# Stores to DRAM scratch moved from SyncE's queue to GpSimd's in two stages of an encoder block

## The chip, the cores and the metric

The kernel runs on one core of a Trainium2 chip. The metric is the device time of one execution in microseconds; the figure given for a kernel is the median over its runs. The engines are called TensorE (PE in the profile, PEld for its weight loads), VectorE (DVE), ScalarE (ACT), GpSimd (POOL) and SyncE (SP). SyncE computes nothing here; it issues DMAs.

## The reference

One layer of a hybrid bidirectional encoder on x of 1 x 1024 x 1024 float32. Branch A is gated linear attention in both directions with 4 heads; branch B is windowed attention with 8 query heads and 2 key heads in blocks of 128. Both are projected, gated and summed, go through W_out, and a SwiGLU block with a hidden width of 2816 follows.

```python
h = _rms_norm(x, norm_mix_g[l])
proj = h @ w_in[l]
(g_q, g_k, g_v, g_r, g_lr_f, g_lr_b, s_q, s_k, s_v, gate_a, gate_b) = jnp.split(proj, split_at, axis=-1)
y_gla = _gla_branch(g_q, g_k, g_v, g_r, g_lr_f, g_lr_b, ...) @ w_o_gla[l]
y_swa = _swa_branch(s_q, s_k, s_v, ...).astype(x.dtype) @ w_o_swa[l]
merged = jax.nn.sigmoid(gate_a) * y_gla + jax.nn.sigmoid(gate_b) * y_swa
x = x + merged @ w_out[l]
h2 = _rms_norm(x, norm_ffn_g[l])
gu = h2 @ w_ffn_in[l]
x = x + (jax.nn.silu(gu[..., :D_FF]) * gu[..., D_FF:]) @ w_ffn_out[l]
```

## The kernel before, in words

Float32 accuracy is had by splitting each operand into a high part (type fp32r, made on ScalarE) and the rest (made on VectorE), and doing three matmuls: high by high, high by low, low by high. So each weight unit of 128 x 512 costs a DMA, a ScalarE copy, a VectorE subtraction and matmuls. Larger products are done by a seven-product scheme on 2 x 2 blocks (the sets 11, 21, 22, T1 to T4), whose operands are sums and differences of blocks. Little stays in SBUF: projections, operand sums and attention outputs are stored to scratch tensors in DRAM and loaded again when they are needed.

The stages in order of time:

- The norm of x, and the first q and k projections (the block from line 352).
- The GLA stage (the block from line 697). `g_gates`, `g_decays`, `g_parts`, `g_scores`, `g_out`, `g_back_out` and `g_turn` work on pairs of 128-token chunks. They load q and k (lines 435, 436) and v (486) from scratch; `g_turn` stores its two transposed heads (594). Between them `fill(n)` draws matmuls from a list of dense projections: `proj_f` (q, k; stored by `proj_f_out`, line 142), `proj_t` (v, and the windowed attention's kv and q; line 227), whose weight units are loaded by `wunit` (65) and, in `wkeep` (162), stored again in split form so that the second half of the tokens can load them in `wagain` (170, 175). `next_unit` keeps AHEAD = 2 units beyond the one in use. In the same time `all_sums` makes operand sums on VectorE and stores them with `put` (116).
- The SWA stage (the block from line 945): `prep`, `a_rope`, `k_turn`, `a_turn`, `a_scores` (the masked scores, 831), `a_soft`, `a_probs` (the transposed probabilities are split into ph and pl, 873 and 874) and `a_out`, which stores the output of four heads through `heads(...)` (885). `heads` is a view of a scratch tensor of 128 x 2048 that picks 128 tokens of each of four heads, so one store writes four rows of 128 numbers per partition. The dense list goes on with `proj_t` and ends with `first_halves` (products of the branch gates, evacuated on VectorE in line 254, stored in 257). When the attention runs out, `drained(t)` loads finished outputs (`b_load`, 892) and makes their sums in place (`b_sum`, 898), which are stored through `heads` too (899). The tiles that `b_load` fills are the attention's own buffers (tags qr, sq, rq, kvr); qr has two.
- The pair stage (line 1123 on), branch projections, W_out and the feed-forward part. Their stores stay where they are.

Order: PE's instructions are issued in the order of the program text (`manual_schedule`). The order on the other engines and queues is made by the framework's planner from its own estimates; a queue then runs in that order, and an instruction that waits holds what stands behind it. All semaphores are set by the framework. Before the change every DMA is issued from SyncE's queue. Staging tiles (`stage()`, tag st) rotate over four buffers, weight tiles wh and wl over five, wr over four; a buffer is written again only when its store has landed. The program reserves scratch for DMAs issued by GpSimd:

```python
nc = _bacc.Bacc("TRN2", target_bir_lowering=False, num_devices=1, dynamic_dma_scratch_size=1024)   # line 1739
```

Of the kernel before, what the change touches and what calls it, by code (L numbers as in the profile page):

```python
# [8 lines left out]
F32 = mybir.dt.float32  # L9
# [5 lines left out]
P = 128  # L15
# [15 lines left out]
def body(tc, i, out):  # L31
    nc = tc.nc
    with ExitStack() as root:
# [12 lines left out]
        def mmtile(shape=(P, 512), dt=F32):  # L46
            return psm.tile(list(shape), dt, tag="mm", name=nm("mm"))
# [4 lines left out]
        def scratch(name, shape=(P, 512)):  # L52
            return dram.tile(list(shape), F32, tag=name, name=name)

        def stage(shape=(P, 512), dt=F32):
            return stg.tile(list(shape), dt, tag="st", name=nm("st"))
# [15 lines left out]
        def mm(o, a, b, start, stop):  # L72
            nc.tensor.matmul(o, a, b, start=start, stop=stop)  # L73
# [36 lines left out]
        xl = [[xp.tile([P, HT], FR, tag=f"xl{k}{s}", name=f"xl{k}{s}") for s in range(2)] for k in range(KT)]  # L110

        scr = {}

        def put(key, t):
            d = scratch("_".join(map(str, key)))
            nc.sync.dma_start(out=d, in_=t)
            scr[key] = d

        swks = ExitStack()
# [13 lines left out]
        def proj_f_out(name, b):  # L133
            for s in range(2):
                d = scratch(f"{name}_{s}")
                t = stage()
                if name[0] == "q":
                    nc.vector.scalar_tensor_tensor(t, b[s], 128 ** -0.5, rstd[:, s * HT:(s + 1) * HT],
                                                   op0=ALU.mult, op1=ALU.mult)
                else:  # L140
                    nc.vector.tensor_tensor(t, b[s], rstd[:, s * HT:(s + 1) * HT], op=ALU.mult)
                nc.sync.dma_start(out=d, in_=t)
                scr[name, s] = d


# [4 lines left out]
        def next_unit():  # L150
            while plan and len(ready) <= AHEAD:
                ready.append(plan.pop(0)())
            return ready.pop(0)
# [3 lines left out]
        def wkeep(n, k):  # L157
            h, l = wunit(i["w_t"][n, k])
            kept[n, k] = []
            for v, q in ((h, "h"), (l, "l"))[n < 2:]:  # L160
                d = dram.tile([P, 512], F32, tag=f"w{q}{n}_{k}", name=f"w{q}{n}_{k}")
                nc.sync.dma_start(out=d, in_=v.bitcast(F32))
                kept[n, k].append(d)
            return h, l

# [31 lines left out]

        def proj_t(name, n, s):
            plan.extend((lambda k=k: (wkeep, wagain)[s](n, k)) for k in range(KT))

            def steps():
                if True:
                    b = [mmtile() for _ in range(4)]
                    us = []

                    def unit_mm(k, t):
                        h, l = us[k]
                        c = slice(t * P, (t + 1) * P)
                        st, sp = k == 0, k == KT - 1
                        for x, w, f0, f1 in ((xh, h, st, False), (xh, l, False, False), (xl, h, False, sp)):  # L210
                            mm(b[t], x[k][s][:, c], w, f0, f1)
                            yield

                    for ks in ((0, 1), (2,), (3,), (4,), (5,)):
                        us.extend(next_unit() for _ in ks)
                        for t in range(4):
                            for k in ks:
                                yield from unit_mm(k, t)
                    us.extend(next_unit() for _ in range(2))
                    for t in range(4):  # L220
                        yield from unit_mm(KT - 2, t)
                        yield from unit_mm(KT - 1, t)
                        ti = s * 4 + t
                        d = scratch(f"{name}_{ti}")
                        o = stage()
                        nc.scalar.activation(o, b[t], AF.Copy, scale=rstdt[:, ti:ti + 1])
                        nc.sync.dma_start(out=d, in_=o)
                        scr[name, ti] = d
            return steps()

# [3 lines left out]
        def first_halves():  # L234
            for j in range(0, len(PAIRS), 2):
                for u in range(2):
                    plan.extend((lambda r=PAIRS[j + q][2], u=u: wunit(i["w_f"][r, u])) for q in range(2))

            def steps():
                for j in range(0, len(PAIRS), 2):  # L240
                    Y = [mmtile(), mmtile()]
                    for u in range(2):
                        for q in range(2):
                            nme, m = PAIRS[j + q][:2]
                            h, l = next_unit()
                            for kk in range(4):
                                k = u * 4 + kk
                                c = slice(kk * P, (kk + 1) * P)
                                for w, x, f0, f1 in ((h, xh[k][0], k == 0, False), (h, xl[k][0], False, False),
                                                     (l, xh[k][0], False, k == KT - 1)):  # L250
                                    nc.tensor.matmul(Y[q], w[:, c], x, start=f0, stop=f1, skip_group_check=True)  # L251
                                    yield
                            t = stage()
                            nc.vector.tensor_tensor(t, Y[q], rstd[:, 0:HT], op=ALU.mult)
                            key = (f"{nme}{m}", 0) if u else (f"{nme}{m}", "p1")
                            d = scratch("_".join(map(str, key)))
                            nc.sync.dma_start(out=d, in_=t)
                            scr[key] = d
            return steps()

# [2 lines left out]
        def fill(n):  # L263

            while n > 0 and dense:
                try:
                    next(dense[0])
                    n -= 1
                except StopIteration:
                    dense.pop(0)  # L270
# [315 lines left out]
        def g_turn(hd, c):  # L586
            a = gla.pop((hd, c))
            ot = chtile((P, 2, P))
            for j in range(2):
                nc.tensor.transpose(ot[:, j], a.ob[:, j * P:(j + 1) * P], ident)  # L590
            os_ = gtile("ot", (P, 2, P))
            nc.scalar.copy(os_, ot)
            for j in range(2):
                nc.sync.dma_start(out=scr["o", 2 * hd + j, c // 4][:, (c % 4) * P:(c % 4 + 1) * P], in_=os_[:, j])

        dense += [proj_t("v0", 0, 0), proj_t("v0", 0, 1), proj_f("q1", 2), proj_f("k1", 3), proj_f("q2", 4), proj_f("k2", 5),
                  proj_t("v1", 1, 0), proj_t("v1", 1, 1), proj_f("q3", 6), proj_f("k3", 7), *(proj_t(nme, n, s) for s in range(2)
# [86 lines left out]
        for n in range(NH * NC):  # L684
            hd, c = divmod(n, NC)
# [9 lines left out]
                behind[n + 1] = (g_parts, hd, c)  # L695
        sums = all_sums()
        with tc.manual_schedule(engines={mybir.EngineType.PE}):
            fill(44)
            for t in range(last + 1):
                work = [[at[t, j]] for j in (0, 5, 4, 3, 2, 1) if (t, j) in at]  # L700
                if t in behind:
                    work = work or [[]]
                    work[-1].append(behind[t])
                if t < 22 and work:
                    work[(len(work) - 1) // 2].append((next, sums, None))
                slot([lambda v=v: [f(*a) for f, *a in v] for v in work], share(GF, t))
                next(sums, None)
# [37 lines left out]
        def heads(q, n):  # L745
            return groups[q].rearrange("p (h t) -> p h t", h=4)[:, :, n % 4 * P:(n % 4 + 1) * P]
# [130 lines left out]
        def a_out(g, n):  # L877
            a = att.pop((g, n))
            o = chtile((P, 4, P))
            for kb, ph, pl in a.pts:  # L880
                mm3(o, vSh[kb][:, g * P:(g + 1) * P], vSl[kb][:, g * P:(g + 1) * P], ph, pl,
                    kb == a.b0, kb == a.b1)
            ob = stage((P, 4, P))
            nc.scalar.copy(ob, o)
            nc.sync.dma_start(out=heads(f"b{g + 1}{n // 4 + 1}", n), in_=ob)

        loaded = {}

# [5 lines left out]
        def b_sum(n, *js):  # L894
            a, b, c, d = loaded[n]
            for j in js:
                q, t, x, y = (("bT1", b, b, a), ("bT2", c, c, b), ("bT3", a, c, a), ("bT4", d, d, c))[j]
                nc.vector.tensor_tensor(t, x, y, op=ALU.subtract)
                nc.sync.dma_start(out=heads(q, n), in_=t)

        def drained(t):
            if t in (0, 2):
# [30 lines left out]
        for n in range(2 * KT):  # L933
            t, g = divmod(n, 2)
# [10 lines left out]
        with tc.manual_schedule(engines={mybir.EngineType.PE}):  # L945
            for t, v in enumerate(todo):
# [5 lines left out]
                if a_scores in names:  # L952
                    pin = a_turn in names and t < 5
                    k = names.index(a_turn) if pin else max(j for j, f in enumerate(names) if f is a_scores)
                    g = v[names.index(a_scores)]
# [165 lines left out]
                 (("12", 1), ("sum2", 3)), (("22", 1), ("21", 1)), (("11", 2),), (("12", 2), ("22", 2)), (("21", 2), ("11", 3)), (("12", 3), ("22", 3)), (), ())  # L1121

        with tc.manual_schedule(engines={mybir.EngineType.PE}):
            homes["T2"] = tp, "t2h{}", "t2l{}", 0
            for k in range(4):
                if k == 2:
# [12 lines left out]
            for j in range(0, len(PAIRS), 2):  # L1139
# [4 lines left out]
                v = [pair_T3(f) for f in two]  # L1144
# [606 lines left out]
```

## Time and profile before

| | |
|---|---|
| median of 3 runs | 1605.99 us (1605.62 to 1606.2) |
| the profiled execution | 1604.61 us |
| its span, first to last instruction | 1602.7 us |
| busy: PE, PEld, DVE, ACT, POOL | 1589.7, 1320.6, 1245.9, 928.4, 0.2 us |
| granted clock of TensorE | 1.00 |
| moved by DMA | 349.47 MB, 218 GB/s over the span |

In the profile L12 is line 12 of the kernel; a tile is named without its buffer number; "out<-in" says what an instruction writes and reads. An instruction of SyncE's queue is written SPq. Matmuls overlap, so a single one's duration is longer than the time from one to the next. "Landing" is the time from the issue of a DMA to the arrival of its semaphore.

### The profile page before, as it was taken

How to read it: one execution, taken by the hardware profiler on the slowest of the kernel's cores; microseconds unless marked ns; L12 is line 12 of the kernel's file. 1: busy time of each engine (PE TensorE's matmuls, PEld its weight loads, DVE VectorE, ACT ScalarE, POOL GpSimd, SP SyncE). 2: the span in 40 equal slices, each digit the busy share in tenths (PEclk: the TensorE clock that was granted, in tenths of full speed). 3: DMA queues.
4: the chain of work that ended last, by engine and by line, in shares of the span. 5: the costliest groups of instructions: out<-in, count | busy, mean ns of one | idle time of the engine just before them, and what ended most of it. 6: DMA issues, size and time to landing. Idle time of an engine off the chain costs nothing.

```text
span 1602.7 us, 23256 instructions
## 1 busy us (share of the span) xinstructions
PE 1589.7 (99%) x7484; PEld 1320.6 (82%) x7484; DVE 1245.9 (78%) x2355; ACT 928.4 (58%) x1911; POOL 0.2 (0%) x4
## 2 busy tenths in 40 slices
PE   9999999999999999999999999999999999999999
PEld 6888888887888788888888888888888888888887
DVE  8578898837899878876877987777777878689655
ACT  7555877864998745445665647844444444354442
POOL 0000000000000000000000000000000000000000
PEclk9999999999999999999999999999999999999999
DMA  7888877888555798877876777634344554695433
GB/s 263 294 273 266 267 250 261 279 273 296 176 155 152 242 301 292 285 239 262 277 232 211 229 219 219 197 113 150 112 150 153 194 200 164 207 331 174 150 99 118
DMA packets 223900, 349.47 MB, mean 218 GB/s; under 512 B 24255, under 2 KB 67135, under 8 KB 223778
## 3 DMA queue, kind: packets, MB, share of 16 engines
q1 hardware_dynamic: 223778, 347.99, 66.6%
q8 instruction: 59, 0.97, 0.3%
q14 instruction: 63, 0.52, 0.1%
HBM read 235.17 MB, written 112.73 MB: 217 GB/s over the span
## 4 chain that ended last, share of the span: by engine, by line
PE 80%; DVE 7%; DMA 7%; ACT 4%; issue 1%; SPq 1%; DVEq 0%; ACTq 0%
PE mm L996 10%; PE mm L997 10%; PE mm L998 10%; PE mm L73 10%; PE mm L1589 7%; PE ch L1589 6%; PE ch L996 6%; PE ch L998 6%; PE ch L997 6%; PE ch L73 4%; PE mm L251 3%; DMA wr<-in_w_t_dram 1%; DMA wr<-in_w_f_dram 1%; PE ch L870 1%; DVE wl L69 1%
## 5 line engine op out<-in xcount | busy, mean ns | idle before, releaser
L975 ACT ACTIVATE wh<-ws 128x512 fp32r<-128x512 f32 x164 | 103.1, 630 | 150.7 <-PE mm L997 75.2
L73 PE MATMUL mm<-wh,xl 128*128 128x512 f32 x320 | 127.2, 398 | 0.0
L73 PE MATMUL mm<-wh,xh 128*128 128x512 f32 x320 | 126.8, 396 | 0.2 <-ACT lrt L318 0.2
L73 PE MATMUL mm<-wl,xh 128*128 128x512 f32 x320 | 127.1, 397 | 0.0
L976 DVE TENSOR_TENSOR wl<-ws,wh 128x512 fp32r<-128x512 f32 x164 | 111.9, 685 | 11.8 <-ACT wh L975 11.7
L975 ACT ACTIVATE wh<-a 128x512 fp32r<-128x512 f32 x66 | 41.6, 632 | 90.1 <-PE ch L1589 42.3
L975 ACT ACTIVATE wh<-wr 128x512 fp32r<-128x512 f32 x96 | 60.0, 628 | 45.6 <-PE ch L997 15.0
L69 DVE TENSOR_TENSOR wl<-wr,wh 128x512 fp32r<-128x512 f32 x98 | 67.0, 684 | 19.8 <-ACT wh L67 19.8
L976 DVE TENSOR_TENSOR wl<-a,wh 128x512 fp32r<-128x512 f32 x66 | 45.6, 690 | 40.8 <-ACT wh L975 40.5
L67 ACT ACTIVATE wh<-wr 128x512 fp32r<-128x512 f32 x98 | 61.1, 628 | 26.0 <-PE mm L73 10.2
L976 DVE TENSOR_TENSOR wl<-wr,wh 128x512 fp32r<-128x512 f32 x96 | 65.4, 685 | 10.0 <-ACT wh L975 9.8
L73 PEld LDWEIGHTS mm<-wh,xh 128*128 128x128 f32 x320 | 60.2, 188 | 10.6 <-ACT lrt L318 0.7
L1589 PE MATMUL mm<-hh,wl 128*128 128x512 f32 x176 | 68.6, 390 | 0.0
L1589 PE MATMUL mm<-hl,wh 128*128 128x512 f32 x176 | 68.5, 389 | 0.0
L1589 PE MATMUL mm<-hh,wh 128*128 128x512 f32 x176 | 68.5, 389 | 0.0
L73 PEld LDWEIGHTS mm<-wl,xh 128*128 128x128 f32 x320 | 60.2, 188 | 9.6
L73 PEld LDWEIGHTS mm<-wh,xl 128*128 128x128 f32 x320 | 60.3, 188 | 9.0
L989 DVE TENSOR_TENSOR ws<-wr,wr 128x512 f32<-128x512 f32 x80 | 54.5, 686 | 10.9 <-DMA wr<-in_w_out_dram 5.1
L1556 DVE TENSOR_TENSOR hl<-hr,hh 128x512 fp32r<-128x512 f32 x77 | 52.8, 685 | 4.7 <-ACT hh L1555 4.7
L996 PE MATMUL mm<-S0h,wh 128*128 128x512 f32 x136 | 52.9, 389 | 0.0
L997 PE MATMUL mm<-S0l,wh 128*128 128x512 f32 x136 | 52.9, 389 | 0.0
L996 PE MATMUL mm<-S1h,wh 128*128 128x512 f32 x136 | 52.9, 389 | 0.0
(444 smaller groups left out, 4945.6 us busy)
## 6 DMA issues: line engine op xcount, KB each, us to landing
wr<-in_w_fi_dram SPq DMA_DIRECT2D x110, 256.0 KB, 3.8
wr<-in_w_f_dram SPq DMA_DIRECT2D x96, 256.0 KB, 3.8
wl<-wl SPq DMA_DIRECT2D x80, 256.0 KB, 3.2
wr<-in_w_t_dram SPq DMA_DIRECT2D x56, 256.0 KB, 3.9
wh<-wh SPq DMA_DIRECT2D x48, 256.0 KB, 3.6
B<-c SPq DMA_DIRECT2D x44, 256.0 KB, 2.0
T<-st SPq DMA_DIRECT2D x44, 256.0 KB, 2.9
a<-in_w_fo_dram SPq DMA_DIRECT2D x44, 256.0 KB, 5.3
```

The lines of the kernel that those rows point to most:

```text
L67: nc.scalar.activation(h, raw, AF.Copy)
L69: nc.vector.tensor_tensor(l, raw, h.bitcast(F32), op=ALU.subtract)
L73: nc.tensor.matmul(o, a, b, start=start, stop=stop)
L251: nc.tensor.matmul(Y[q], w[:, c], x, start=f0, stop=f1, skip_group_check=True)
L975: nc.scalar.activation(h, src, AF.Copy)
L976: nc.vector.tensor_tensor(l, src, h.bitcast(F32), op=ALU.subtract)
L989: nc.vector.tensor_tensor(t, x, y, op=op)
L996: nc.tensor.matmul(o, h[:, c], x[kk][0], start=start and kk == 0, stop=False, skip_group_check=True)
L997: nc.tensor.matmul(o, h[:, c], x[kk][1], start=False, stop=False, skip_group_check=True)
L998: nc.tensor.matmul(o, l[:, c], x[kk][0], start=False, stop=kk == nk - 1, skip_group_check=True)
L1556: nc.vector.tensor_tensor(l, r, h.bitcast(F32), op=ALU.subtract)
L1589: nc.tensor.matmul(ys[m], a[:, c], b, start=f0, stop=f1, skip_group_check=True)
```

## The change

A one-element list `via` holds the queue, and a helper `keep` issues a store on it. All stores to scratch of the first two stages go through `keep`. `via` is set to GpSimd's queue just before the loop of the GLA stage and back to SyncE's at the start of the pair stage, so the stores traced in between, those of the GLA and the SWA stage, are issued by GpSimd. Loads are not touched. The stores ahead of the GLA stage (the first q and k) and those from the pair stage on stay on SyncE's queue.

```diff
@@ -110,10 +110,14 @@
         scr = {}
+        via = [nc.sync]
+
+        def keep(d, t):
+            via[0].dma_start(out=d, in_=t)
 
         def put(key, t):
             d = scratch("_".join(map(str, key)))
-            nc.sync.dma_start(out=d, in_=t)
+            keep(d, t)
             scr[key] = d
@@ proj_f_out
-                nc.sync.dma_start(out=d, in_=t)
+                keep(d, t)
@@ wkeep
-                nc.sync.dma_start(out=d, in_=v.bitcast(F32))
+                keep(d, v.bitcast(F32))
@@ proj_t
-                        nc.sync.dma_start(out=d, in_=o)
+                        keep(d, o)
@@ first_halves
-                            nc.sync.dma_start(out=d, in_=t)
+                            keep(d, t)
@@ g_turn
-                nc.sync.dma_start(out=scr["o", 2 * hd + j, c // 4][:, (c % 4) * P:(c % 4 + 1) * P], in_=os_[:, j])
+                keep(scr["o", 2 * hd + j, c // 4][:, (c % 4) * P:(c % 4 + 1) * P], os_[:, j])
@@ the GLA stage's loop
         with tc.manual_schedule(engines={mybir.EngineType.PE}):
+            via[0] = nc.gpsimd
             fill(44)
@@ a_out
-            nc.sync.dma_start(out=heads(f"b{g + 1}{n // 4 + 1}", n), in_=ob)
+            keep(heads(f"b{g + 1}{n // 4 + 1}", n), ob)
@@ b_sum
-                nc.sync.dma_start(out=heads(q, n), in_=t)
+                keep(heads(q, n), t)
@@ the pair stage
         with tc.manual_schedule(engines={mybir.EngineType.PE}):
+            via[0] = nc.sync
             homes["T2"] = tp, "t2h{}", "t2l{}", 0
```

## The prediction

> **What bounds the kernel now.** I read the page first, then the busy time by stretches, then who makes TensorE wait, then what the queues do just ahead of those waits.
>
> ```profile
> span 1602.7 us, 23256 instructions
> PE 1589.7 (99%) x7484; PEld 1320.6 (82%) x7484; DVE 1245.9 (78%) x2355; ACT 928.4 (58%) x1911; POOL 0.2 (0%) x4
> q1 hardware_dynamic: 223778, 347.99, 66.6%
> ```
>
> TensorE is busy for all but 13.0 us of the span. GpSimd is empty, and one hardware queue, SyncE's, carries nearly all packets. The profiled execution took 1604.61 us for its span of 1602.7 us; the median of the three runs is 1605.99 us, 1.4 us more. I make the sum against the span and add what comes out to the median.
>
> The next view has a line for each stretch: from, to and length, then the busy time of each engine with its instructions, the granted clock, the DMA share and the rate. The stretches are my cuts: the norm and first projections, the linear attention (GLA, to about 380), the windowed attention (SWA), its drained end, and all that follows.
>
> ```profile
> 0.00:42.00 42.00, 40.01 (x167) 28.98 (x168) 34.77 (x55) 29.98 (x46) 0.20 (x4) 1.00 0.78 263
> 42.00:380.00 338.00, 334.58 (x1795) 283.37 (x1794) 253.60 (x579) 227.94 (x595) 0.00 (x0) 1.00 0.83 272
> 380.00:515.00 135.00, 133.70 (x721) 114.52 (x720) 121.47 (x347) 119.13 (x292) 0.00 (x0) 1.00 0.58 182
> 515.00:566.00 51.00, 48.90 (x259) 40.53 (x258) 40.72 (x107) 34.90 (x85) 0.00 (x0) 1.00 0.78 239
> 566.00:1603.00 1037.00, 1032.48 (x4549) 853.18 (x4548) 795.30 (x1271) 516.44 (x894) 0.00 (x0) 1.00 0.62 202
> ```
>
> The clock is 1.00 throughout. The changed stores lie in the second, third and fourth lines. TensorE's first column falls short of the length there by 3.42, 1.30 and 2.10 us. So **6.8 us is all that a perfect change could gain**, and 2.1 us of it lies in the 51 us in which the windowed attention runs out. There TensorE waits for:
>
> ```profile
> PE ch L73 <- DVE pl L874: 2.1, 3, 0.9
> PE ch L73 <- DVE sql L817: 1.0, 1, 1.0
> PE ch L73 <- DVE ob L571: 0.9, 1, 0.9
> ```
>
> No row names a DMA: a late transfer reaches TensorE only by holding VectorE or ScalarE, each of which works in order.
>
> **The change part by part.** (1) SyncE loses the stores of both mixers. By the loops these are in the GLA stage 48 operand sums (line 116), 64 kept weight halves (162), 64 head outputs (594), 16 tiles of v (227) and 12 of q and k (142), 204 together; then 24 projection tiles (227), 16 attention outputs (885), 12 sums of those (899) and about 20 first halves (257). Here is what they cost SyncE. A wait row has the total, the number of times and the longest; an issue row has the smallest, median and largest ns of the instruction, and the row at its end is the time from issue to landing.
>
> ```profile
> SPq L227 <- ACT st L226: 24.4, 19, 4.1
> SPq L257 <- DVE mx L846: 12.9, 4, 4.6
> SPq L116 <- DVE xn L606: 12.2, 12, 2.1
> SPq L257 <- DVE st L254: 9.1, 6, 2.7
> SPq L594 <- ACT ot L592: 7.8, 8, 3.1
> ...
> L116 SPq DMA_DIRECT2D xT<-xn x16: 319/320/420, 164.0 to 320.8; - x16
> L594 SPq DMA_DIRECT2D o<-ot x64: 319/423/2129, 174.0 to 359.7; - x64
> ...
> L885 SPq DMA_DIRECT2D b<-st x16: 512/519/631, 414.4 to 562.3; - x16
> DMA to landing us min/median/max: 2.9/3.3/3.8
> ...
> L899 SPq DMA_DIRECT2D bT<-qr x8: 518/558/702, 521.3 to 562.9; - x8
> DMA to landing us min/median/max: 2.6/3.8/4.3
> ```
>
> The five wait rows are 66.4 us in which SyncE stood before a store whose data was not there, with loads queued behind it. Those loads now start sooner, each by a few us at most. What it is worth: TensorE does not wait for loads in these rows, and its idle time in the two long stretches is 3.42 + 1.30 = 4.7 us, most of it ended by VectorE or ScalarE finishing a piece of the recurrence. Bounds 0 and -4.7 us; I take 0, because no row of TensorE's waits has a load as releaser. The cover is the dense projections that fill each step.
>
> (2) GpSimd's queue gains them. The trace has no DMA issued by GpSimd, so its time for one store is bounded by SyncE's rows: 0.32 us from below (a plain store's issue) and 3.3 us from above (one store landed before the next is begun). In the GLA stage 204 stores in 338 us leave 1.66 us for each. Below that the queue keeps up on average. I take a value near the lower end, as an issue is what SyncE's rows measure too, and cost the GLA stage at 0. Work that covers a store that lands 1 or 2 us later: AHEAD = 2 weight units of 12 matmuls each lie ready, and stage tiles rotate over four buffers.
>
> (3) The order of stores among themselves stays, and each still waits for its data. What is queued behind a waiting store is now only other stores. Loads that read a scratch buffer, and writers that reuse a staging tile, wait for landings as before.
>
> (4) **The drained end, 515 to 566, is where I place the cost.** Here 18 of the stores are of another kind. Lines 885 and 899 write through heads(), four rows of 128 numbers in each partition, 512 separate rows of 512 bytes where a plain store has 128 of 2 KB. SyncE needs 519 and 558 ns to issue one against 320 ns. The next lines are SyncE's queue, then VectorE's wait for qr in this stretch (total, times, longest), then VectorE and TensorE, in order of time:
>
> ```profile
> 539.55 0.56 SPq L885 DMA_DIRECT2D b<-st  x1
> 540.57 0.56 SPq L899 DMA_DIRECT2D bT<-qr  x1
> 541.18 0.65 SPq L899 DMA_DIRECT2D bT<-rq  x1
> 541.92 0.59 SPq L257 DMA_DIRECT2D ga<-st  x1
> 542.60 1.48 SPq L899 DMA_DIRECT2D bT<-qr  x2
> 544.12 0.83 SPq L899 DMA_DIRECT2D bT<-sq  x1
> 546.09 1.92 SPq L892 DMA_DIRECT2D qr<-b  x3
> 548.11 0.58 SPq L899 DMA_DIRECT2D bT<-kvr  x1
> ...
> DVE qr L898 <- DMA qr<-b: 4.0, 2, 3.4
> ...
> 551.16 0.69 DVE L898 TENSOR_TENSOR qr<-qr 128x512 f32<-128x512 f32 x1 [3.35 <-DMA qr<-b]
> 552.65 0.66 DVE L874 TENSOR_TENSOR pl<-mm,ph 128x512 fp32r<-128x512 f32 x1
> ...
> 553.36 0.50 PE L73 MATMUL ch<-pl,vSh 128*128 128x512 f32 x1 [0.93 <-DVE pl L874]
> ```
>
> Read it backwards. TensorE is idle for 0.93 us before 553.36, until VectorE's pl. VectorE was idle for 3.35 us before 551.16, until the load of qr. That load goes into the buffers from which bT was stored, so it waits for those stores to land. There is no slack anywhere on this path: **a us by which the bT stores land later is a us of the kernel.**
>
> How much later? Bound from below: as on SyncE, several four-head stores in flight, 0 us (an earlier landing could give back at most the 2.1 us of this stretch). Bound from above: one at a time. From 539.55 the four-head stores in line are b, bT, bT, bT, bT. At 3.3 us each the fourth has landed at 539.55 + 13.2 = 552.75 and the fifth at 556.05. The loads that wait for them went out from 546.09 and the last of the three by 548.0, so they move by 6.7 to 8.1 us. At the smallest landing, 2.9 us, the fourth is done at 551.15, a delay of 5.1 us; at 3.8 us the fifth is done at 558.55, 10.6 us. I take one at a time for these 18 stores, and 8 us for it, with 5 to 14 us as this case's own range (14: the stores of lines 885 and 899 between 521.3 and 562.9 are 18 x 3.3 = 59.4 us in a window of 41.6 us that ended at about 566, so the last is about 14 us late). The reason for that end: the program reserves 1024 bytes of scratch for GpSimd's DMAs (line 1739), a small room, and these stores have four times the pieces; SyncE's rows already show that pieces cost. The plain stores I leave at the lower bound.
>
> By the Trainium skill (DMA: Bandwidth & Descriptors, sections "SWDGE vs HWDGE vs iDMA" and "The descriptor swizzle") GpSimd writes its descriptors, 16 bytes each, into rings in a reserved piece of SBUF, and a plain 128-partition transfer is eight data descriptors and one of completion on each DMA engine. By those figures 1024 bytes would be 64 descriptors (my estimate), seven plain stores at 9 but only one four-head store at 33. By the page the sum would be the upper bound, 8 us; by SyncE's rows alone, 0. No row of this trace can show which.
>
> (5) After 566 nothing changes its queue. Buffers that the SWA pools give back are reused there, and the stores still in line hold four stage tiles; dense projection work on TensorE lies over it. I cost that at 0, with the 14 us above as its bound.
>
> Sum: 0 + 0 + 0 + 8 + 0 = +8 us, 1605.99 + 8 = **1614 us**.
>
> **The rivals.**
>
> *Nothing to be seen (within 0.2%, 3.2 us, which is about what a measurement of this kernel can tell from no change).* The stores land at most a us or so later, four-head stores overlap, and the path at 553 moves by that us. For it: 99% busy, and no DMA among the releasers. Against it: the path without slack at 553. Time 1606.
>
> *Faster.* SyncE's freed queue sends loads sooner, and VectorE's waits for loads shrink; then pl, sql and ob are earlier. It decides from the point at which more than 3.2 of the 6.8 us idle goes, so it needs both the long stretches and the drained end. For it: 66.4 us of SyncE's waits. Against it: the 2.1 us of the end hang on stores, not on the order of the queue. Time 1605.99 - 4.5 = about 1601.5, and not below 1599.2.
> The Trainium skill (the same page, "Issuing engines are not separate DMA queues") says that issuing from several engines only saves the sequencer's issue time, as all run on the same 16 DMA engines. By that rule the gain would be SyncE's issue time, which no row here has TensorE waiting for: 1606.
>
> *GpSimd is the bound of the GLA stage.* If a plain store takes it more than 1.66 us, stores pile up over 338 us: at 1.75 us by 204 x 1.75 - 338 = 19 us. Kept weights then hold their five buffers and stage tiles their four, and TensorE runs dry. For it: nothing but the upper bound of 3.3 us. Against it: SyncE's 0.32 us. With the drained end on top, about 1606 + 19 + 8 = 1633.
>
> **How the numbers follow.** Four-head stores one at a time, +5 to +14 us, 1611 to 1620: 0.47. GpSimd as the bound of GLA, slower still: 0.13. Nothing to be seen: 0.26. Faster: 0.14. So slower 0.47 + 0.13 = 0.60, same 0.26, faster 0.14. The range reaches into the faster case at 1602 (a gain of 4) and to the saturated case at 1632, which leaves out about 0.1 on each side; the likeliest case's own range is 1611 to 1620.
>
> **What would show it right or wrong.** Right: in the changed profile a queue of GpSimd carries the mixers' stores; gaps of about 3 us between GpSimd's issues of lines 885 and 899 after 515 us, not between plain stores; VectorE's wait for qr<-b grows from 4.0 us in total to about 12; TensorE's idle time in that stretch grows by about 8 us while the GLA stretch keeps its 3.4 us. The prediction is wrong if the four-head stores follow each other within a us (then nothing, or a gain), if the idle time appears before 380 us (then the plain stores were mis-sized), or if another order of work on VectorE, which the planner derives anew, takes the qr sums off the path.

## The result, and the profile after

The changed kernel takes 1640.4 us (median of 5 runs, 1638.15 to 1642.07), the kernel before 1605.99 us (5 runs beside them): ratio 1.0216, 95% interval 1.0205 to 1.0228. It is 34.4 us slower, where 8 were forecast. Lines of the profile after are 4 to 6 higher than those of before (885 is 890, 898 is 903, 874 is 879); all of GpSimd's stores have the helper's line, 116.

From the page of the changed kernel:

```profile
span 1638.6 us, 23486 instructions
PE 1599.9 (98%) x7484; PEld 1325.2 (81%) x7484; DVE 1247.6 (76%) x2355; ACT 930.5 (57%) x1911; POOL 155.4 (9%) x280
q1 hardware_dynamic: 173282, 288.20, 55.2%
q0 software_dynamic: 19008, 59.79, 9.7%
```

The stores did move: a second queue has 59.79 MB, and GpSimd is busy for 155.4 us. TensorE's idle time grew from 13.0 to 1638.6 - 1599.9 = 38.7 us, and its busy time, for the same matmuls, by 10.2 us, most of it the clock's (see the part on why the prediction was wrong).

Both traces have 7484 matmuls in the same order, so the start of the n-th one in each can be compared. The difference is the lag:

| at this time in the kernel before (us) | 129 | 346 | 531 | 567 | 594 | 1599 |
|---|---|---|---|---|---|---|
| lag of the changed kernel (us) | 4.2 | 7.5 | 9.3 | 20.9 | 34.7 | 35.6 |

So **9.3 us are lost before the drained end, 11.6 us in it (531 to 567), 13.8 us just behind it, and nearly nothing after that**. The busy times by stretch say the same (from, to, length, busy time of PE, PEld, DVE, ACT and POOL, granted clock, DMA share, rate):

```profile
42.00:380.00 338.00, 330.17 (x1763) 279.46 (x1761) 247.94 (x564) 224.36 (x587) 116.45 (x214) 0.99 0.80 266
380.00:515.00 135.00, 133.18 (x702) 111.93 (x701) 120.16 (x343) 113.56 (x280) 17.37 (x29) 1.00 0.58 191
515.00:566.00 51.00, 45.98 (x242) 38.07 (x241) 37.82 (x108) 37.55 (x94) 10.40 (x16) 0.93 0.46 145
566.00:620.00 54.00, 37.96 (x157) 30.14 (x157) 29.13 (x48) 19.19 (x36) 9.20 (x15) 0.87 0.72 246
620.00:1638.00 1018.00, 1013.08 (x4464) 837.08 (x4462) 778.21 (x1241) 505.71 (x873) 0.00 (x0) 1.00 0.62 199
```

TensorE's idle time in the GLA stretch went from 3.42 to 7.83 us, and between 566 and 620 it idles for 16.0 us. GpSimd is busy for 116 of 338 us in the GLA stage: it is no bound there. What TensorE waits for:

```profile
PE mm L255 <- DVE st L258: 12.6, 2, 11.0
PE ch L73 <- DVE pl L879: 7.8, 3, 3.6
PE ch L73 <- ACT th L545: 3.1, 3, 1.8
PE ch L594 <- DVE ob L575: 2.2, 1, 2.2
```

The two upper rows are the end of the SWA, the two lower ones the GLA. Ahead of the upper ones GpSimd's queue does this (start, duration; b and bT are four-head stores, ga and gb plain ones; in brackets the idle time before):

```profile
555.94 0.72 POOL L116 DMA_DIRECT2D bT<-qr  x1 [3.90 <-DVE st L258]
558.92 0.71 POOL L116 DMA_DIRECT2D bT<-rq  x1 [2.26 <-issue]
559.54 0.62 POOL L116 DMA_DIRECT2D ga<-st  x1
561.95 0.72 POOL L116 DMA_DIRECT2D bT<-qr  x1 [1.79 <-DVE mx L851]
...
576.54 0.71 POOL L116 DMA_DIRECT2D bT<-qr  x1 [2.27 <-DVE pl L879]
579.52 0.72 POOL L116 DMA_DIRECT2D b<-st  x1 [2.27 <-issue]
580.16 0.62 POOL L116 DMA_DIRECT2D ga<-st  x1
...
592.91 0.72 POOL L116 DMA_DIRECT2D bT<-qr  x1 [5.48 <-issue]
595.90 0.71 POOL L116 DMA_DIRECT2D bT<-qr  x1 [2.27 <-issue]
598.88 0.72 POOL L116 DMA_DIRECT2D b<-st  x1 [2.27 <-issue]
```

A four-head store follows another after 2.98 us or more, with some 2.3 us of idle time before it, mostly "issue", that is, a wait for nothing that the trace names; a plain store follows 0.62 us behind. How this comes to TensorE, in order of time:

```profile
570.08 0.69 DVE L903 TENSOR_TENSOR qr<-qr 128x512 f32<-128x512 f32 x1 [7.59 <-DMA qr<-b]
...
572.29 0.50 PE L73 MATMUL ch<-pl,vSh 128*128 128x512 f32 x1 [3.43 <-DVE pl L879]
...
598.73 1.15 ACT L922 ACTIVATE t2h<-xn 128x512 fp32r<-128x512 f32 x2 [14.49 <-DMA bT<-qr]
...
599.39 1.29 DVE L923 TENSOR_TENSOR t2l<-xn,t2h 128x512 fp32r<-128x512 f32 x2 [7.59 <-ACT t2h L922]
...
601.80 0.68 DVE L258 TENSOR_TENSOR st<-mm,rstd 128x512 f32<-128x512 f32 x1
```

The first pair is the path that the prediction drew. The rest is one that it did not: the pair stage's first tile t2h lies where the attention's buffers were, so ScalarE stands for 14.49 us until the last bT store has landed (issued at 595.90); VectorE stands behind ScalarE for 7.59 us; and behind that in VectorE's order stands the evacuation of line 258, for which TensorE stands for 11.0 us.

### The profile page after: what moved, and what is told of

The parts are those of the page before. It is cut to its first block, busy times and chain, and to the rows that moved or that the text cites. A ratio compares the mean times of both kernels' runs of the same rounds, so it can differ in the third digit from the quotient of the medians.

```text
span 1638.6 us, 23486 instructions
## 1 busy us (share of the span) xinstructions
PE 1599.9 (98%) x7484; PEld 1325.2 (81%) x7484; DVE 1247.6 (76%) x2355; ACT 930.5 (57%) x1911; POOL 155.4 (9%) x280
## 3 DMA queue, kind: packets, MB, share of 16 engines
q0 software_dynamic: 19008, 59.79, 9.7%
## 4 chain that ended last, share of the span: by engine, by line
PE 71%; issue 9%; DVE 8%; DMA 6%; POOL 3%; ACT 2%; SPq 0%; POOLq 0%; DVEq 0%; ACTq 0%
PE mm L1001 9%; PE mm L1002 9%; PE mm L1003 9%; PE mm L1595 7%; PE mm L73 7%; PE ch L1595 5%; PE ch L1001 5%; PE ch L1003 5%; PE ch L1002 5%; PE ch L73 5%; PE mm L255 2%; DMA b<-st 1%; DVE wl L981 1%; DMA kvr<-skv 1%; DMA qr<-sq 1%
## 5 line engine op out<-in xcount | busy, mean ns | idle before, releaser
L67 ACT ACTIVATE wh<-wr 128x512 fp32r<-128x512 f32 x98 | 61.0, 627 | 14.8 <-PE mm L73 10.6
```

Source lines behind the costliest of these rows:

```text
L67: nc.scalar.activation(h, raw, AF.Copy)
```

## Experiments: the end of the SWA

Theory R: four-head stores go one at a time through GpSimd's queue because its scratch has no room for two. The first four kernels ran beside the kernel before at 1604.62 us; each ratio is to the kernel before beside it.

**Only the four-head stores back in SyncE's queue.**

```diff
-            keep(heads(f"b{g + 1}{n // 4 + 1}", n), ob)
+            nc.sync.dma_start(out=heads(f"b{g + 1}{n // 4 + 1}", n), in_=ob)
-                keep(heads(q, n), t)
+                nc.sync.dma_start(out=heads(q, n), in_=t)
```

> The changed kernel with only the four-head stores (the attention's head sums and its operands' sums, four rows to a partition) back in SyncE's queue; the GLA's stores stay in GpSimd's. Theory R (the end of the SWA loses its 25 us because GpSimd's queue takes four-head stores one at a time, one each 3 us): the lag behind the kernel before stays about 9 us up to the 541st us and the 25 us behind it go, so 1615 us (1612 to 1618), and the 11 us wait of DVE's L258 for the pair stage's t2h is gone. Rival O (all that costs is the planner's new order, or that every GpSimd store lands later): no single kind of store carries it, the time stays above 1630.

Measured: 1615.1 us, ratio 1.0062 (1.0043 to 1.0081). The lag is 7.3 us at 531, 7.8 at 567 and 10.2 at 594: the loss of the end is gone but for 2.9 us, and the GLA's is not.

**Only the four-head stores in GpSimd's queue** (those of the first two stages; `via` stays SyncE's).

```diff
-            via[0] = nc.gpsimd
+            via[0] = nc.sync
-            keep(heads(f"b{g + 1}{n // 4 + 1}", n), ob)
+            nc.gpsimd.dma_start(out=heads(f"b{g + 1}{n // 4 + 1}", n), in_=ob)
-                keep(heads(q, n), t)
+                (nc.gpsimd if n < 3 else nc.sync).dma_start(out=heads(q, n), in_=t)
```

> Only the four-head stores of GLA and SWA in GpSimd's queue, every plain store in SyncE's as before. Theory R: they go 3 us apart with no plain store beside them too, the last 25 us of the SWA are lost as in the changed kernel and the GLA's 9 us are not, so 1631 us (1626 to 1636). Rival B (a backlog: it is the plain stores of the GLA in the same queue that hold the four-head stores up): with the plain stores gone the queue is free and the time is within 3 us of 1606.

Measured: 1631.12 us, ratio 1.0159 (1.0135 to 1.0182). The lag is -1.6 us at 531, 13.7 at 567, 24.1 at 594. GpSimd's queue holds nothing else here, and the distances are the same:

```profile
544.98 0.71 POOL L904 DMA_DIRECT2D bT<-qr  x1 [3.22 <-DVE qr L903]
548.01 0.71 POOL L904 DMA_DIRECT2D bT<-rq  x1 [2.32 <-issue]
551.00 0.71 POOL L904 DMA_DIRECT2D bT<-sq  x1 [2.27 <-DVE mx L851]
553.98 0.72 POOL L904 DMA_DIRECT2D bT<-qr  x1 [2.27 <-issue]
```

So these 28 stores cost 26.5 us alone, and the plain ones 10.5 us alone; together 34.4.

**More scratch.** Everything else, the order of each engine's instructions too, is that of the changed kernel.

```diff
-PAD = 672
+PAD = 32
-    ... dynamic_dma_scratch_size=1024)
+    ... dynamic_dma_scratch_size=1664)
```

> The changed kernel with 1664 bytes of GpSimd's DMA scratch instead of 1024; the 640 bytes come off a filler tile, so that every other buffer has the same place and size. Theory R with the scratch as what makes the stores wait (it holds one four-head store and a few plain ones, with 1664 bytes some three four-head ones): their issues come about 0.7 us apart (their own busy time) instead of 3.0, most of the 25 us of the end go, the 9 us of the GLA stay: 1616 us (1612 to 1622). Rival S (the 3.0 us are what GpSimd needs for each four-head store whatever the scratch holds): the distances stay 3.0 us and the time 1638 to 1642.

Measured: 1616.92 us, ratio 1.0075 (1.0051 to 1.0099). The lag is 3.6 us at 531, 4.1 at 567, 8.8 at 594. GpSimd's queue:

```profile
543.62 0.71 POOL L116 DMA_DIRECT2D b<-st  x1 [4.96 <-ACT st L889]
544.48 0.72 POOL L116 DMA_DIRECT2D bT<-qr  x1
545.12 0.82 POOL L116 DMA_DIRECT2D bT<-rq  x1
546.67 0.56 POOL L116 DMA_DIRECT2D ga<-st  x1 [0.73 <-DVE rd L862]
547.58 1.55 POOL L116 DMA_DIRECT2D bT<-qr  x2 [0.35 <-DVE pl L879]
```

Three four-head stores start within 1.5 us (543.62 to 545.12). The distance was the room's, not GpSimd's own. The Trainium skill (DMA: Bandwidth & Descriptors, sections "Terms" and "The descriptor swizzle") gives 16 bytes for a descriptor and 9 descriptors of each side (read and write) on each DMA engine for a plain transfer. Worked out from it as an estimate, counting one side as the prediction did, 64 descriptors hold one four-head store of 33 and up to three plain ones, and 104 hold three four-head ones. The traces agree: a plain store 0.62 us behind a four-head one with 1024 bytes, the next four-head one 2.98 us behind, three in a row with 1664.

R expected the GLA's 9 us to stay, and in this trace 3.6 us of lag are left of them, with VectorE and ScalarE in the order of the changed kernel. Part of the difference is the clock: it is 1.00 here over the GLA stage, where the changed kernel's trace has 6.9 us at 0.51 (shown below). What the rest is was not measured; the control's trace, next, is 2.8 us early at 346 us.

**Control: all stores in SyncE's queue, 1664 bytes.**

> Control: the kernel before (all these stores in SyncE's queue) with the same 1664 bytes of scratch. It puts nothing new in GpSimd's queue, so each theory expects 1606 us within 2 us; if it is faster or slower than that, the scratch itself moves the time and the run with 1664 bytes is to be read against this one.

Measured: 1603.31 us, ratio 0.999 (0.9979 to 1.0001). The scratch by itself moves nothing that can be told. Its trace lags by -2.8 us at 346 and -4.5 at the end, so lags of two traces are not read closer than about 4 us here.

**The stores of the last group alone back in SyncE's queue** (the kernel before beside it: 1604.26 us).

```diff
-                keep(heads(q, n), t)
+                (nc.sync if n == 2 else via[0]).dma_start(out=heads(q, n), in_=t)
```

> The changed kernel with only the four bT stores of the third group of heads (the last that are issued before the pair stage) back in SyncE's queue. Theory R for the hand-over: the 11 us that TensorE waits for the pair stage's first t2h are the landing of those last stores, which come at the end of GpSimd's row of one each 3 us; the lag at the 567th us stays about 21, and the 14 us behind it shrink to 0 to 4: 1628 us (1625 to 1632). Rival T (the earlier four-head stores, already 3 us apart and late, hold the buffers as well): the stall stays, above 1634.

Measured: 1630.83 us, ratio 1.0164 (1.0147 to 1.0181), inside R's range. The lag is 17.5 us at 567 and 23.7 at 594, so of 13.8 us behind the drained end 6.2 are left, more than the 0 to 4 that R expected. TensorE's waits between 515 and 620:

```profile
PE ch L73 <- DVE pl L879: 9.2, 3, 4.7
PE mm L255 <- ACT mm L1022: 4.2, 1, 4.2
```

The 11.0 us behind VectorE's st are gone, and 4.2 us behind a later ScalarE copy are next. The hand-over of the buffers to the pair stage is therefore held by these four stores for most of its time, and the waits for pl come of the earlier ones.

## Experiments: the GLA's 10 us

Theory L: the stores of operand sums land later, so the three xn tiles and the single pwh and pwl come back later, and VectorE, which takes the sums in program order, stands on their loads. In the trace of the kernel with the four-head stores back, SyncE stands before the load into xn for a store to land, and VectorE before the load (182 to 192, and 42 to 220 us):

```profile
SPq L606 <- DMA xT<-xn: 5.2, 1, 5.2
...
DVE xn L615 <- DMA xn<-in_xT_dram: 3.5, 1, 3.5
```

In the kernel before, 168 to 190 us, the first of these was

```profile
SPq L602 <- DMA xT<-xn: 1.8, 2, 1.6
```

Rival O: the planner makes a new order when stores change their queue, and that order costs the time.

**The operand sums back too, and the operand sums alone.** The first differs from the 1615 us kernel by one line of `put`; the second is the kernel before with that line alone.

```diff
             d = scratch("_".join(map(str, key)))
-            keep(d, t)
+            nc.sync.dma_start(out=d, in_=t)      # the second: nc.gpsimd up to the pair stage
```

> The kernel that took 1615.1 us (four-head stores back in SyncE's queue) with the stores of the GLA's operand sums (bs, bs4, wo, xT, x) back there too; GpSimd keeps the plain stores of projections, kept weight halves, o and the attention's ga. Theory L (the 9 us of the GLA: an operand sum lies in one of three xn tiles or in the single pwh and pwl, DVE takes the sums in program order, and a store from GpSimd hands its tile back later, so the ring turns slower and DVE stands on a load with the scan's steps behind it): the 9 us go, 1606 us (1603 to 1609). Rival O (the planner's new order of DVE and ACT costs them; most of that order stays here): 1612 to 1616.

> Only the stores of the GLA's operand sums in GpSimd's queue, every other store in SyncE's as in the kernel before. Theory L: 5 to 9 us are lost on these alone, up to the 380th us, by DVE's waits for xn and pwl: 1613 us (1610 to 1616). Rival Q (it is the company in GpSimd's queue that holds the sums up: v, o and the weight halves ahead of them): alone they pass, 1606 us within 2.5 us.

Measured: 1614.83 us, ratio 1.0063 (1.0051 to 1.0075), with the sums back; 1612.26 us, ratio 1.0049 (1.0037 to 1.0061), with the sums alone. The first contradicts L: it is no faster than the kernel with the sums on GpSimd. The second is what L expected. So each half alone (10.6 and 8.0 us) costs about what both cost (10.5), which a sum of store delays does not explain. It fits O, if the new orders that these moves give happen to cost alike; that they do is not shown, and for the second kernel L stands, as it was not run in the old order. The kernel with only the four-head stores on GpSimd speaks for O too: its VectorE has the old order up to the end of the SWA, and its lag at 531 is -1.6 us.

**Both remedies.** The changed kernel with 1664 bytes and that line of `put`.

> The changed kernel with both remedies: 1664 bytes of scratch and the operand sums back in SyncE's queue; the four-head stores stay in GpSimd's. If the room of the scratch and the sums' ring are all that the change costs, what is left are the 3 to 5 us of the end of the SWA that the kernel with 1664 bytes still lost: 1609 us (1606 to 1612). If something else holds (the planner's order, the later landing of all other stores), it stays at the 1617 us of that kernel, or above 1613.

Measured: 1619.24 us, ratio 1.0095 (1.0076 to 1.0115), well above the 1609 expected. The sums' way back adds nothing to what the room alone gave (ratio 1.0075).

**The order held.** In the last four kernels (the kernel before beside them: 1604.23 us) edges of order without a wait were added, so that VectorE, ScalarE, SyncE and GpSimd issue in the order that the planner had made for another kernel, given as a list of the instructions' numbers:

```diff
+    for queue in orders:                      # lists of numbers, by queue
+        last = {}
+        for n in queue:
+            i = traced.get(f"I-{n}")
+            if i.engine in last:
+                tc.add_manual_dep(i, last[i.engine].name, mybir.DependencyInfo(
+                    mybir.DependencyClass.NoSync, mybir.DependencyReason.DATA), reason="order")
+            last[i.engine] = i
```

With the plain stores on GpSimd and the four-head ones on SyncE, in the order of the kernel before:

> The 1615 us kernel (plain stores in GpSimd's queue, four-head stores in SyncE's) in the order of the kernel before. Theory O: 1605 us (1602 to 1608); below 1604 only if the loads that no longer wait behind stores bring something. Rival L: 1612 to 1616, as in the planner's order.

Measured: 1607.42 us, ratio 1.0026 (1.0015 to 1.0036). Of 10.5 us 3.2 are left, so 7.3 went with the order. TensorE's busy time between 42 and 206 us, in the planner's order:

```profile
42.00:206.00 164.00, 157.13 (x806) 132.57 (x805) 117.53 (x248) 98.77 (x234) 41.54 (x76) 0.98 0.79 266
```

and in the order of the kernel before, with the same stores on GpSimd:

```profile
42.00:206.00 164.00, 160.69 (x840) 135.07 (x840) 121.97 (x257) 101.24 (x238) 41.98 (x77) 1.00 0.81 269
```

In the old order TensorE is busy for 3.6 us more. The clock differs too: in the planner's order it was 0.50 from 114.9 to 118.3 us and from 196.8 to 200.2 (0.98 over the row), in the old order 1.00. So part of the 7.3 us is not idle time but work at half the clock behind slightly longer waits. VectorE's wait for the load from in_xT is now

```profile
DVE xn L615 <- DMA xn<-in_xT_dram: 0.5, 1, 0.5
```

The opposite: all stores on SyncE, VectorE and ScalarE in the order made for the 1615 us kernel.

> The opposite of it: every store in SyncE's queue as before, DVE and ACT held to the order that the planner made for the 1615 us kernel. Theory O: the order alone loses 6 to 11 us: 1613 us (1610 to 1617). Rival L: with the stores prompt the order is harmless, 1606 us within 2.5 us.

Measured: 1626.06 us, ratio 1.0139 (1.012 to 1.0158), slower than either expected. The lag is 4.6 us at 346, which the order costs with prompt stores too, and 17.0 at 531. The second part is not VectorE's and ScalarE's order alone, with which the 1615 us kernel loses 0.3 us between 380 and 415 us. SyncE's order was left to the planner, and in these 35 us ScalarE stood on one load:

```profile
ACT sq L780 <- DMA qr<-sq: 10.6, 1, 10.6
```

So this run bounds the order's part in the GLA stage only.

The whole change in the order of the kernel before:

> The change alone, with every other effect of a new plan taken out: the changed kernel, its DVE, ACT, SyncE and GpSimd held by added edges of order (no waits) to the order that the planner gave the kernel before; the stores stand in GpSimd's queue in the order they had in SyncE's. Theory O (the GLA's 9 us come of the planner's new order, which sets the operand sums' steps closer behind their loads): the lag at the 515th us is under 3 us, the 25 us of the SWA's end stay: 1631 us (1627 to 1634). Rival L (they come of the stores' later landing in an unchanged ring of tiles): the 9 us stay, 1638 to 1642.

Measured: 1635.38 us, ratio 1.0208 (1.0181 to 1.0234), between the two ranges, and its interval does not tell it from the changed kernel's. Its lag does: 1.7 us at 531, as O expected, where the changed kernel has 9.3. The end then loses 10.5 us up to 567 and 16.4 behind it; TensorE's longest wait there is

```profile
PE mm L255 <- ACT wh L980: 13.2, 1, 13.2
```

so some of what the old order saves in the GLA stage the old order of the end gives back.

The same with 1664 bytes of scratch:

> All stores in GpSimd's queue as changed, but with 1664 bytes of scratch and in the order of the kernel before. If order and room are the whole cost: 1608 us (1604 to 1611), with the 3 to 5 us that the SWA's end still lost with 1664 bytes. If something third holds: 1613 or more, near the 1617 us that the room alone gave.

Measured: 1611.84 us, ratio 1.005 (1.0034 to 1.0066), just above the range expected of order and room. The lag is 0.2 us at 531, 1.8 at 567, 3.8 at 594. Order and room take away 26.8 of 34.4 us; 7.6 us are left. The end of the SWA, which even here waits 3.5 us for pl and 1.7 us for a wh, has some of them, and later landings may have others; how they divide was not measured. No variant was faster than the kernel before by more than its interval.

## Why the prediction was wrong

By its own steps:

- **(4), the drained end, was right.** Four-head stores go one each 3 us, plain stores do not, and the cause is the room that it named. Expected 8 us (5 to 14), measured 11.6 as a lag, of which 2.7 are the clock's (below). VectorE's wait, said to grow from 4.0 to about 12 us:

```profile
DVE qr L903 <- DMA qr<-b: 10.8, 4, 7.6
```

- **(5), behind 566, failed.** It was costed at 0, with 14 us as its bound and dense work as its cover; it measured 13.8. That the bound has the same size is in part luck, as the wait itself is 11.0 us and 2.7 are the clock's. The last store was worked out to be about 14 us late, and the working stopped there, without asking who writes first into the buffers that it frees. That is ScalarE's t2h, and VectorE's evacuation for the dense products stands behind it in order, so the cover itself ran dry. The row to look for was the next stage's first write into the SWA pools.
- **(2), the GLA stage, failed in size, not in its reason.** One store takes GpSimd 0.54 us, as near SyncE's 0.32 as assumed, and the queue keeps up; the rival with GpSimd as bound fell. The 0 was wrong by 9.3 us all the same. Part of that is an effect that no step had as a term: the planner's new order. By the run in the old order 7.3 of 10.5 us are its cost with 1024 bytes and the four-head stores on SyncE; but the trace with 1664 bytes has the new order too and lags by only 3.6 us at 531, so the order's share of the 9.3 us stays open. 3.1 of them are the clock's. The prediction named a new order only as something that could take the qr sums off the path. 3.2 us are left with the order held. Later landings may be their cause, but that is not shown: at the median o and xT land after 2.2 us before and 3.5 after, v only after 3.6 and 4.0, bs after 3.2 and 3.4, and xT takes 3.2 us also where SyncE issues the sums again.
- **(1), the freed loads, was right at 0; that they start sooner is not shown.** ScalarE's waits for weight loads between 42 and 220 us are gone after, and TensorE gained nothing. It was not the freed queue that took them away: they are there again with the same plain stores on GpSimd and the old order held. Before, and then with the old order:

```profile
ACT wh L67 <- DMA wr<-in_w_f_dram: 7.6, 4, 3.0
ACT wh L172 <- DMA wr<-in_w_t_dram: 5.3, 3, 2.4
...
ACT wh L67 <- DMA wr<-in_w_f_dram: 9.9, 3, 4.8
ACT wh L176 <- DMA wr<-in_w_t_dram: 2.3, 2, 1.8
```

The rule of the Trainium skill (DMA: Bandwidth & Descriptors, section "Issuing engines are not separate DMA queues") gave 1606 us; as far as the gain goes the trace agrees, but with the old order held and the four-head stores on SyncE the kernel is still 3.2 us slower, so another issuing engine was not neutral here.
- **Not in the sum at all: the clock.** Of 35.9 us in the span 10.2 are busy time. The clock fell three times in the changed kernel's trace: 0.9 us behind TensorE's wait of 2.2 us in the GLA stage, and during its waits of 3.6 and 11.0 us at the end of the SWA. The three stretches at half the clock, and then the way back behind the long wait:

```profile
195.00:201.90 6.90, 6.28 (x24) 5.10 (x23) 5.39 (x13) 6.22 (x19) 2.28 (x5) 0.51 0.51 149
556.80:563.70 6.90, 5.30 (x16) 4.44 (x17) 5.12 (x18) 3.67 (x12) 1.97 (x3) 0.51 0.43 136
594.40:608.00 13.60, 5.37 (x13) 4.25 (x14) 7.11 (x12) 6.19 (x11) 2.51 (x4) 0.50 0.73 250
...
602.50:604.50 2.00, 1.87 (x5) 1.51 (x6) 2.00 (x4) 1.09 (x2) 0.00 (x0) 0.50 1.01 389
606.50:608.50 2.00, 2.00 (x7) 1.53 (x7) 2.00 (x4) 1.62 (x3) 0.00 (x0) 0.61 1.11 355
608.50:610.50 2.00, 2.00 (x10) 1.63 (x9) 2.00 (x4) 0.00 (x0) 0.00 (x0) 1.00 1.06 373
```

Behind the wait TensorE does 5 and 7 matmuls in 2 us, at a clock of 0.50 and 0.61, where it does 10 at 1.00. Half of TensorE's busy time in the three stretches is what the clock adds, as an estimate 3.1 us to the GLA's loss, 2.7 to the drained end's and 2.7 to the one behind it: 8.5 of the 10.2 us. In this trace a us of waiting came to about 1.4 us: 35.9 of span for 25.7 of idle time.

## What to carry to other kernels

Before DMAs move to GpSimd's queue, see how many of their pieces its scratch holds at once: where only one store fits, they run one after the other, and 640 bytes more took away 22 of 34 us here. When a chain of stores gets late, follow it past the stage's last instruction to the first write into each buffer that it frees, and to what stands behind that write on its engine. Where a planner orders the work, a moved instruction is also a new order; hold the old one by edges to see which of the two costs. And where TensorE is the bound, add to each wait of 2 us or more the work that may follow it at half the clock.

## What the runs showed of the hardware that was not expected

- The granted clock fell not only with a wait of 11.0 us but also behind one of 2.2 us, and it came back 5.4 us behind the end of the long one (602.6 to 608.0). Not each such wait does it: in the kernel with both remedies the clock stays at 0.99 to 1.00 through a wait of 2.9 us that ends at 578.6. The Trainium skill (TensorE: Matmul & The Clock Gate, section "Part 1: The HAM clock gate (the "warmup" mystery)") says that the clock is halved after an idle window of about 3.4 us and full again around 4 us into steady work; the trace agrees in the half (0.50), but here it fell behind a wait of 2.2 us too, and the way back took 5.4 us.
- GpSimd issues a plain store in 0.54 us and a four-head one in 0.72 us, SyncE in 0.32 and 0.52. A queue that has no room for the next store mostly shows its wait as "issue", with no releaser named.
